# A two-block kernel whose expert stage runs in program order, gathers rows and streams through 22 tiles

## The chip, the core and the metric

One NeuronCore of a Trainium2 chip runs the whole program in one launch. The metric is device microseconds per execution: 1643.91 us in the median of 3 runs (1638.96 to 1644.89). The traced execution took 1639.19 us, 1637.3 us of it between its first and its last instruction (the span); every time of the trace below counts from the span's start.

## The reference

256 tokens of 1024 float32 numbers pass through two different blocks.

```python
# first block
u = rmsnorm(h) @ w_in;  h = h + concat(stick_breaking(u), rwkv7(u)) @ w_out
xn = rmsnorm(h)
# hier_moe: 1 of 4 groups by softmax, then 2 of its 8 experts, 32 experts in all
for e in range(32):
    y = y + combine[:, e:e+1] * ((silu(xn @ w_gate[e]) * (xn @ w_up[e])) @ w_down[e])
x = rmsnorm(h + y)
# second block, two layers of
x = x + 0.5 * swiglu(rms_norm(x), ffn1_w_gate, ffn1_w_up, ffn1_w_down)     # 1024 -> 2816 -> 1024
x = x + concat(ssd(...), mla(...), conv(...)) @ w_out
x = x + 0.5 * swiglu(rms_norm(x), ffn2_w_gate, ffn2_w_up, ffn2_w_down)
```

An expert's three weights are 1 MB each (1024x256, 1024x256, 256x1024), so the expert stage reads 96 MB.

## The kernel before

`Front` does the first block's mixers, `Moe` the experts, `Block2` the second block. Five engines run their own instruction lists: TensorE (PE, with its weight loads PEld), VectorE (DVE), ScalarE (ACT), GpSimd (POOL) and SyncE (SP), which issues the weight loads. The framework's scheduler orders each list by its own estimates. Instructions issued through `K.V`, `K.S`, `K.T` (class `InOrder`), or through `K.engines()` and `K.mm` while `K.ordered` is true, keep the order of the program text instead.

**Experts (`Moe.run`).** Each expert has room for 32 tokens (CAP), and four experts form a quad, so a quad's 4 x 32 places fill 128 partitions. `OH[j]` holds, for token half j, which token sits in which place (0 or 1). The 8 quads q go through these steps:

- gather: `gather(q, j, b)` multiplies token columns (stationary, every 8th column of `x`) by `OH` (moving, 128 columns), which gives the tokens of the quad already transposed; 16 matmuls a quad, each two instructions in the trace. `gathered(b)` scales them out of PSUM into `XG0` (DVE) and `XG1` (ACT, four pieces).
- `up(a, q, hf)`: 32 matmuls a half for the gate (hf 0) and for the up part (hf 1); k is the outer loop and the expert i the inner one, so that four neighbouring matmuls fill four different 32-column strips of the array.
- `act`: SiLU (ACT), times up and weight (DVE), two transposes (PE), copy to `hT` (ACT).
- `down(q, hT)`: 16 matmuls over two 512-column halves n, expert i outside, k inside.
- `back(q, ys, n)`: the result, split into `yh` (ACT) and `yl` (DVE), goes back to the tokens through `OHT` into four accumulators `py`. `slots_T` makes `OHT` for two quads at once, at even q.

Quad 0 also computes the routing weights (`weights`: 16 pairs of small matmuls on `cw` for all quads), `beyond` counts the fullest expert, and at q == 2 every engine branches on that count (`all_tokens`, not taken here).

**The ring.** `load_next` issues the 96 weight loads of 1 MB in order from SP (L1046, L1051, L1054): a quad's 4 gates, 4 ups, 4 downs. They go into NRING = 20 tiles; load n needs the tile of load n - 20 to be free. The first 20 wait only until `Front` gives its memory up; load 20 waits for `up(0)`'s gate half, and so on. A load also waits until the one 8 places before it has landed. `spare` takes ring tiles again for late use (`fg`, `fsq`, `yr`). Only the routing and quad 0 up to `act` are in program order (`K.ordered`).

**Gate/up of the second block (`Block2.ffn`, L1713).** Weights come as units of two 128-row slices k with 512 columns (256 gate, 256 up), split into `wh` (ACT) and `wl` (DVE). For every output half b and s (gate, up), `K.mm` issues two matmuls of `wh` with 512 moving columns and two of `wl` with 256: long, long, short, short, four times a unit. There are 10 such i with 4 units in each of 4 FFNs: 160 units, 1280 long and 1280 short matmuls.

Of the kernel before, what the change touches and what calls it, by code (L numbers as in the profile page):

```python
# [9 lines left out]
F32 = mybir.dt.float32  # L10
# [3 lines left out]
OP = mybir.AluOpType  # L14
# [939 lines left out]
        router.rest = [acs[1, n] for n in range(2)]  # L954


NRING = 20
BIG = 1e30


class Moe:
# [52 lines left out]
    def run(self, ctx, x, B=None):  # L1014
# [98 lines left out]
            return [lambda: K.V.tensor_add(rank[:, j], negm[:, j], pr[:, j]), lambda: place(j, 0, 4)]  # L1113


        XG, pg = [None, None], [None, None]
# [9 lines left out]
        def gathered(b):  # L1126
            XG[b] = wk.tile([P, 4, P], F32, name=f"XG{b}")
            if b == 0:
                K.V.tensor_mul(XG[b], pg[b], gp[:, 0:4, None].to_broadcast([P, 4, P]))
            else:  # L1130
                for k in range(4):
                    S.activation(XG[b][:, k], pg[b][:, k], AF.Copy, scale=gp[:, 4 + k:5 + k])
        OHT = [None]

        def slots_T(q):
            OHT[0] = wk.tile([P, 2, T], F32R, name="OHT")
            pt = K.mx.tile([P, 2, T], F32, name="mx")
            for i in range(2):
                for j in range(2):
                    nc.tensor.transpose(pt[:, i, j * P:(j + 1) * P],  # L1140
                                        OH[j][:, 4 * (q + i):4 * (q + i) + 4].rearrange("p e c -> p (e c)"), K.ident)
            S.activation(OHT[0], pt, AF.Copy)  # L1142

        def quads(t):
# [3 lines left out]
        def weights():  # L1148
            def t(name, n=1):
                return K.sm.tile([P, 2, n], F32, name=name, bufs=1)  # L1150
            eg, gs, p2, w1 = t("weg", 4), t("wgs"), t("wp2"), t("ww1")
            l32 = lm.rearrange("p j g e -> p j (g e)")
            K.V.tensor_sub(eg, lg[:, :, 0:4], mg.to_broadcast([P, 2, 4]))
            K.V.tensor_sub(p2, v8[:, :, 1:2], v8[:, :, 0:1])
            K.V.tensor_sub(l32, l32, v8[:, :, 0:1].to_broadcast([P, 2, NE]))
            S.activation(eg, eg, AF.Exp)
            S.activation(p2, p2, AF.Exp)
            S.activation(l32, l32, AF.Exp)
            V.tensor_reduce(gs, eg, axis=AX.X, op=OP.add)
# [6 lines left out]
            V.tensor_mul(comb, quads(mask), quads(l32))  # L1166
            for j in range(2):
                for q in range(8):
                    K.mm(pw[:, q], OH[j][:, 4 * q:4 * q + 4].rearrange("p e c -> p (e c)"), cw[:, j, q], j + q == 0, j == 1, share=True)
            V.tensor_mul(own, own, pw[:, :, 0:4])  # L1170
            V.tensor_reduce(ws[:, 0:8], own, axis=AX.X, op=OP.add)
            V.tensor_copy(ws[:, 8:16], pw[:, :, 4])


        def beyond():
# [49 lines left out]
        def down(q, hT):  # L1225
            ys = []
            for n in range(2):
                y = K.mx.tile([P, 512], F32, name="mx")
                for i in range(4):
                    for k in range(2):  # L1230
                        K.mm(y[32 * i:32 * i + 32], hT[:, k, 32 * i:32 * i + 32],
                             W["d", 4 * q + i, 0][:, k, n * 512:(n + 1) * 512], k == 0, k == 1)
                ys.append(y)
            return ys

# [10 lines left out]

        def back(q, ys, n):
            if q == 7 and n:
                t = spare("yr", 2, F32R)
# [34 lines left out]
        gather(0, 0, 0)  # L1284
        run(ranks(1))
        gather(0, 1, 0)
        gather(0, 0, 1)
        gathered(0)
        gather(0, 1, 1)
        for j in range(2):  # L1290
            place(j, 4, NE)
        def next_rows(q):
            for b in range(2):
                for j in range(2):
                    gather(q, j, b)
                gathered(b)

        for q in range(NE // 4):
            if q == 2:
                all_tokens(nmax)  # L1300
            if q == 2:
                next_rows(q)
            a = K.mx.tile([P, 1024], F32, name="mx")
            if q == 0:
                gathered(1)
            up(a, q, 0)
            load_next(4)
            if q == 7:
                fg = spare("fg", 17)
                src = A["final_norm_g"]  # L1310
                nc.gpsimd.dma_start(fg, bass.AP(tensor=src.tensor, offset=src.offset, ap=[[0, P], [1, D]]))
            up(a, q, 1)
            load_next(4)
            if q == 0:
                weights()
                nmax = beyond()
# [8 lines left out]
            if q == 0:  # L1325
                next_rows(1)
                K.ordered = False
            if q == 0:
                with_x(1, 1)
            if q == 7 and B:  # L1330
                next(par, None)
            y = down(q, hT)
            load_next(4)
            for n in range(1 if q == 7 else 2):
                back(q, y, n)


        V, S = K.V, K.S
        st = K.sm.tile([P, 2, 2, 2], F32, name="fst", bufs=1)
        a1 = K.sm.tile([P, 2], F32, name="fa", bufs=1)  # L1340
        sq = spare("fsq", 18)
        half = [slice(n * 512, (n + 1) * 512) for n in range(2)]

        def square(j, n):
# [37 lines left out]
    def act(self, wk, a, w, r):  # L1382
        K, nc = self.K, self.nc
        sg = wk.tile([P, 256], F32, name="msg")
        hT = wk.tile([P, 2, P], F32, name="mhT")
        nc.scalar.activation(sg, a[:, 0:256], AF.Silu, scale=r)
        nc.vector.scalar_tensor_tensor(sg, a[:, 256:512], w, sg, op0=OP.mult, op1=OP.mult)
        for k in range(2):
            nc.tensor.transpose(a[:, 512 + k * P:512 + (k + 1) * P], sg[:, k::2], K.ident)
        nc.scalar.activation(hT, a[:, 512:768].rearrange("p (k t) -> p k t", k=2), AF.Copy)  # L1390
        return hT


# [19 lines left out]
class Block2:  # L1413
# [258 lines left out]
    def ffn(self, ctx, x, first=None):  # L1672
# [40 lines left out]
        for i in range(1, FF // 256):  # L1713
            ac = sums(i)
            for wh, wl, k0, m in self.units(("gu", i), 0, KD):
                for b in range(2):
                    for s in range(2):
                        c = slice(s * 256 + b * P, s * 256 + (b + 1) * P)
                        for k in range(m):
                            K.mm(ac[b][s], wh[:, k, c], X[:, k0 + k], k0 + k == 0, False, share=True)  # L1720
                        for k in range(m):
                            K.mm(ac[b][s][:, 0], wl[:, k, c], X[:, k0 + k, 0], False, k0 + k == KD - 1, share=True)
# [615 lines left out]
```

## Time and profile before

| | |
|---|---|
| traced execution, and its span | 1639.19 us, 1637.3 us |
| PE busy | 1585.5 us, 97% of the span |
| DVE, ACT busy | 1032.5 us (63%), 832.0 us (51%) |
| first and last issue of an expert weight load | 163.01 us, 424.53 us |
| first and last matmul on expert weights | 236.85 us, 454.19 us |
| mean granted TensorE clock | 0.984 |

Busy times of PE count a matmul from its start to a modelled end, and matmuls overlap, so a busy PE may still be late or early: the distance from one start to the next is what a matmul takes of the engine. Idle time is listed with the engine that ended it. The transfer rate of each 41 us slice stands in the page's slices; 421 GB/s is the highest, held through three of them.

### The profile page before, as it was taken

To read this page: it belongs to the slowest core of one execution; us is meant where nothing else is said; L and a number is where in the kernel's file an instruction comes from. 1 tells how busy PE (TensorE), PEld (TensorE's weight loads), DVE (VectorE), ACT (ScalarE), POOL (GpSimd) and SP (SyncE) were. 2 spreads that over 40 slices of the span, in tenths; PEclk is the share of its full clock that TensorE was granted. 3 is DMA by queue.
4 is the path that set the end of the run, shared out by engine and by line. 5 is a ranking of instruction groups with operands and counts; after the bars stand their busy time and mean duration, and the time that the engine had idled before them with its cause. 6 is when DMAs were issued, how large, how long until landed. Compare 5 with 4: busy or idle time off the path is not lost.

```text
span 1637.3 us, 25206 instructions
## 1 busy us (share of the span) xinstructions
PE 1585.5 (97%) x9862; PEld 1325.9 (81%) x9862; DVE 1032.5 (63%) x1905; ACT 832.0 (51%) x1400; POOL 43.5 (3%) x134
## 2 busy tenths in 40 slices
PE   8999999999889999999999999999999999999998
PEld 7989875665458888899878888888888989778887
DVE  7876651000177656868987775667658779876753
ACT  6633421111255654668745664456546677555653
POOL 4000000000200000000000000000000000000000
PEclk9999999999999999999999999999999999999999
DMA  6431589999765555643545655566556434555553
GB/s 211 140 93 65 220 314 382 421 421 421 318 217 182 180 190 189 200 155 104 178 164 173 193 183 191 194 191 184 190 187 224 142 108 157 175 169 180 181 194 114
DMA packets 195644, 331.29 MB, mean 202 GB/s; under 512 B 11972, under 2 KB 150674, under 8 KB 183362
## 3 DMA queue, kind: packets, MB, share of 16 engines
q1 hardware_dynamic: 186208, 315.19, 55.5%
q0 software_dynamic: 4528, 13.41, 2.4%
q8 instruction: 78, 1.28, 0.3%
q10 hardware_dynamic: 4786, 1.05, 0.3%
q14 instruction: 44, 0.36, 0.1%
HBM read 328.25 MB, written 1.38 MB: 201 GB/s over the span
## 4 chain that ended last, share of the span: by engine, by line
PE 76%; DVE 3%; ACT 2%; issue 1%; DMA 0%; POOL 0%; ACTq 0%
PE acc L246 39%; PE mx L246 27%; PE acc L48 7%; DVE wl L258 1%; PE mx L48 1%; DVE wl L48 1%; DMA cr<-csd 0%; PE mx L1954 0%; PE mx L1978 0%; ACT wh L277 0%; ACT p L1969 0%; PE mx L2024 0%; ACT fsq L48 0%; ACT X L48 0%; DVE x L1520 0%
## 5 line engine op out<-in xcount | busy, mean ns | idle before, releaser
L258 DVE TENSOR_TENSOR wl<-wr,wh 128x1024 fp32r<-128x1024 f32 x358 | 436.3, 1222 | 255.9 <-ACT wh L277 255.2
L277 ACT ACTIVATE wh<-wr 128x1024 fp32r<-128x1024 f32 x358 | 377.8, 1058 | 335.2 <-PE acc L246 235.5
L246 PE MATMUL acc<-X,wh 128*128 128x256 f32 (+1 forms) x1664 | 396.5, 330 | 0.0
L246 PE MATMUL acc<-X,wl 128*128 128x256 f32 x1152 | 272.5, 282 | 0.0
L246 PEld LDWEIGHTS acc<-X,wh 128*128 128x128 f32 x1664 | 260.1, 191 | 5.3 <-issue 4.2
L246 PEld LDWEIGHTS acc<-X,wl 128*128 128x128 f32 x1152 | 218.5, 190 | 28.5
L246 PE MATMUL mx<-X,wh 128*128 128x512 f32 x640 | 201.6, 396 | 0.0
L246 PEld LDWEIGHTS mx<-X,wl 128*128 128x128 f32 x640 | 120.2, 188 | 28.4
L246 PE MATMUL mx<-X,wl 128*128 128x256 f32 x640 | 125.8, 278 | 0.0
L246 PE MATMUL acc<-wh,hh 128*128 128x512 f32 x288 | 112.1, 389 | 0.0
L246 PE MATMUL acc<-wl,hh 128*128 128x512 f32 x288 | 112.1, 389 | 0.0
L246 PE MATMUL acc<-wh,hl 128*128 128x512 f32 x288 | 112.0, 389 | 0.0
L246 PEld LDWEIGHTS mx<-X,wh 128*128 128x128 f32 x640 | 97.5, 189 | 0.2
L246 PEld LDWEIGHTS acc<-wh,hl 128*128 128x128 f32 x288 | 54.1, 188 | 11.2
L246 PEld LDWEIGHTS acc<-wh,hh 128*128 128x128 f32 x288 | 54.1, 188 | 11.1
L246 PEld LDWEIGHTS acc<-wl,hh 128*128 128x128 f32 x288 | 54.1, 188 | 11.1
L246 PE MATMUL acc<-wh,m 128*128 128x512 f32 x192 | 61.3, 394 | 0.0
L246 PE MATMUL mx<-mw,XG 128*32 128x256 f32 x896 | 58.1, 391 | 0.0
L1254 DVE TENSOR_TENSOR yl<-mx,yh 128x512 fp32r<-128x512 f32 x15 | 10.4, 691 | 75.0 <-ACT yh L1253 75.0
L246 PEld LDWEIGHTS mx<-OH,x 128*128 128x128 f32 x192 | 46.7, 334 | 7.8 <-issue 3.3
L246 PE MATMUL mx<-mw,mhT 128*32 128x512 f32 x256 | 48.3, 622 | 4.6 <-ACT mhT L1390 4.6
L246 PE MATMUL mx<-OH,x 128*128 128x128 f32 x192 | 49.3, 411 | 3.5 <-ACT OHT L1142 1.4
(643 smaller groups left out, 2609.2 us busy)
## 6 DMA issues: line engine op xcount, KB each, us to landing
wr<-in_w_in SPq DMA_DIRECT2D x44, 1024.0 KB, 5.3
wr<-in_ffn_w_gate SPq DMA_DIRECT2D x88, 512.0 KB, 4.0
wr<-in_ffn_w_up SPq DMA_DIRECT2D x88, 512.0 KB, 5.0
wr<-in_ffn_w_down SPq DMA_DIRECT2D x40, 1024.0 KB, 5.0
mw<-in_exp_w_gate SPq DMA_DIRECT2D x32, 1024.0 KB, 19.2
mw<-in_exp_w_up SPq DMA_DIRECT2D x32, 1024.0 KB, 17.8
mw<-in_exp_w_down SPq DMA_DIRECT2D x31, 1024.0 KB, 16.4
wr<-in_w_out SPq DMA_DIRECT2D x20, 1024.0 KB, 4.9
```

What stands on the lines that cost most here:

```text
L48: return lambda *a, **k: self.tc.keep_in_program_order(f(*a, **k))
L246: self.engines()[2].matmul(out, l, r, start=start, stop=stop, skip_group_check=share)
L258: i = self.K.engines()[0].tensor_sub(l, v, h)
L277: self.K.engines()[1].activation(h, v[:, q:q + c], AF.Copy)
L1254: K.engines()[0].tensor_sub(yl, ys[n], yh)
```

## The change

The expert stage stays in program order to its end (`K.ordered = False` moves behind the loop; `act` and `slots_T` go through `K.engines()` and `K.T`). The gather swaps operands: `OH` is stationary and 512 columns of `x` move, four matmuls a quad; `gathered` copies the rows to `xr` (half by ACT, half by DVE), and `rows_T` transposes them (8 PE transposes of every 8th column) and scales them into `XG0`, `XG1`. The gather for quad q + 1 stands ahead of `act(q)`, its `rows_T` behind it. `down` gets k outside and i inside. Quad 0 computes its own routing weights alone (`slot_weights(0, 1)`); the other seven, the count and one `with_x` follow its `down`. The ring has 22 tiles; the software queue's scratch shrinks to 4096 bytes of a partition. The FFN issues, for a unit, all 8 long matmuls and then all 8 short ones.

```diff
-NRING = 20
+NRING = 22
...
-        def gather(q, j, b):
+        def gather(q, j):
             if j == 0:
-                pg[b] = K.mx.tile([P, 4, P], F32, name="mx")
+                pg[0] = K.mx.tile([P, 2, 512], F32, name="mx")
+            for n in range(2):
+                K.mm(pg[0][:, n], OH[j][:, 4 * q:4 * q + 4].rearrange("p e c -> p (e c)"), x[:, j, n * 512:(n + 1) * 512],
+                     j == 0, j == 1, share=True)
+        def gathered():
+            xr[0] = wk.tile([P, 2, 512], F32, name="xr")
+            S.activation(xr[0][:, 0], pg[0][:, 0], AF.Copy)
+            V.tensor_copy(xr[0][:, 1], pg[0][:, 1])
+        def rows_T():
+            pt = K.mx.tile([P, KD, P], F32, name="mx")
+            for k in range(KD):
+                T_.transpose(pt[:, k], r[:, k::KD], K.ident)
...
+            V.tensor_mul(XG[0], pt[:, 0:4], gp[:, 0:4, None].to_broadcast([P, 4, P]))
             for k in range(4):
-                K.mm(pg[b][:, k], x[:, j, 4 * b + k::KD], OH[j][:, 4 * q:4 * q + 4].rearrange("p e c -> p (e c)"),
-                     j + k == 0, j == 1, share=True)
+                S.activation(XG[1][:, k], pt[:, 4 + k], AF.Copy, scale=gp[:, 4 + k:5 + k])
...
-                for i in range(4):
-                    for k in range(2):
+                for k in range(2):
+                    for i in range(4):
                         K.mm(y[32 * i:32 * i + 32], hT[:, k, 32 * i:32 * i + 32],
...
-            if q not in (0, 1, 7):
-                next_rows(q + 1)
+            if q != 7:
+                rows(q + 1)
...
             hT = self.act(wk, a, ws[:, q:q + 1], ws[:, 8 + q:9 + q])
-            if q == 0:
-                next_rows(1)
-                K.ordered = False
+            if q not in (1, 7):
+                rows_T()
...
+            if q == 0:
+                slot_weights(1, 8)
+                nmax = beyond()
+                with_x(1, 1)
...
+                bs = [(ac[b][s], slice(s * 256 + b * P, s * 256 + (b + 1) * P)) for b in range(2) for s in range(2)]
+                for a, c in bs:
+                    for k in range(m):
+                        K.mm(a, wh[:, k, c], X[:, k0 + k], k0 + k == 0, False, share=True)
+                for a, c in bs:
+                    for k in range(m):
+                        K.mm(a[:, 0], wl[:, k, c], X[:, k0 + k, 0], False, k0 + k == KD - 1, share=True)
...
+    nc = bacc.Bacc("TRN2", target_bir_lowering=False, num_devices=1, dynamic_dma_scratch_size=4096)
```

On SP, loads 19 to 22 of the ring before (`waits` names the semaphores: DMAHW of earlier loads, PE, DVE):

```order
L1046 DMA mw<-in_exp_w_up 128x2048 [waits DMAHW2_49]
L1051 DMA mw<-in_exp_w_down 128x2048 [waits DMAHW3_49,PE_49]
L1051 DMA mw<-in_exp_w_down 128x2048 [waits DMAHW4_49,PE_49]
L1051 DMA mw<-in_exp_w_down 128x2048 [waits DMAHW5_49,PE_49]
```

The same four loads of the change:

```order
L1046 DMA mw<-in_exp_w_up 128x2048 [waits DMAHW2_49]
L1051 DMA mw<-in_exp_w_down 128x2048 [waits DMAHW3_49,DVE_49]
L1051 DMA mw<-in_exp_w_down 128x2048 [waits DMAHW4_49]
L1051 DMA mw<-in_exp_w_down 128x2048 [waits DMAHW5_49,PE_49]
```

Loads 20 and 21 no longer wait for PE; the DVE wait of load 20 is for `Front`'s last write in that memory. From load 22 on PE frees the tiles.

On PE, quad 5 before, from its gate/up matmuls (`mw` the weights, `XG` the gathered tokens; `OH_2282`, `OH_2283` the two token halves) to its way back:

```order
L246 MATMUL mx<-mw,XG_3308 32x256 x15
L246 MATMUL mx<-mw,XG_3319 32x256 x16
L246 MATMUL mx<-mw,XG_3308 32x256 x16
L246 MATMUL mx<-mw,XG_3319 32x256 x16
L246 MATMUL mx<-OH_2282,x 128x128 x4
L246 MATMUL mx<-OH_2283,x 128x128 x4
L1389 MATMUL mx<-ident,msg 128x128 x2
L246 MATMUL mx<-mw,mhT 32x512 x16
L246 MATMUL acc<-yh,OHT 128x512 x2
L246 MATMUL acc<-yl,OHT 128x512 x2
```

The same stretch of the change (`xr` the gathered rows):

```order
L48 MATMUL mx<-mw,XG_3327 32x256 x16
L48 MATMUL mx<-mw,XG_3328 32x256 x16
L48 MATMUL mx<-mw,XG_3327 32x256 x16
L48 MATMUL mx<-mw,XG_3328 32x256 x16
L48 MATMUL mx<-x,OH_2288 128x512 x2
L48 MATMUL mx<-x,OH_2289 128x512 x2
L48 MATMUL mx<-ident,msg 128x128 x2
L48 MATMUL mx<-ident,xr 128x128 x8
L48 MATMUL mx<-mw,mhT 32x512 x16
L48 MATMUL acc<-yh,OHT 128x512 x2
L48 MATMUL acc<-yl,OHT 128x512 x2
```

Eight gather matmuls before the `msg` transposes (the other eight stand elsewhere) became four with 512 columns, and eight transposes follow the `msg` transposes.

In `Block2.ffn`, PE before (one and a half of the four (b, s) of a unit):

```order
L246 MATMUL acc<-X,wh 128x512 x2
L246 MATMUL acc<-X,wl 128x256 x2
L246 MATMUL acc<-X,wh 128x512 x2
```

and in the change, a whole unit and the start of the next:

```order
L246 MATMUL acc<-X,wh 128x512 x8
L246 MATMUL acc<-X,wl 128x256 x8
L246 MATMUL acc<-X,wh 128x512 x8
```

The matmuls are the same; the switches between long and short fall from eight to two a unit.

## Rows read from the trace of the kernel before

**Rows 1.** Page: PE's line, and the transfer rate of the 40 slices.
```profile
PE 1585.5 (97%) x9862; PEld 1325.9 (81%) x9862; DVE 1032.5 (63%) x1905; ACT 832.0 (51%) x1400; POOL 43.5 (3%) x134
...
GB/s 211 140 93 65 220 314 382 421 421 421 318 217 182 180 190 189 200 155 104 178 164 173 193 183 191 194 191 184 190 187 224 142 108 157 175 169 180 181 194 114
```

**Rows 2.** Busy by stretch: PE, PEld, DVE, ACT, POOL; then clock, DMA share, GB/s.
```profile
235.00:240.00 5.00, 4.27 (x41) 3.07 (x44) 2.49 (x12) 2.07 (x8) 0.00 (x0) 1.00 0.25 103
240.00:245.00 5.00, 5.00 (x100) 3.02 (x96) 0.03 (x1) 0.00 (x0) 0.00 (x0) 1.00 0.40 111
...
250.00:255.00 5.00, 4.29 (x13) 2.92 (x14) 1.23 (x6) 1.92 (x3) 0.00 (x0) 0.50 1.01 424
...
260.00:265.00 5.00, 5.00 (x35) 3.24 (x38) 0.00 (x0) 1.14 (x4) 0.00 (x0) 1.00 0.74 306
265.00:270.00 5.00, 4.78 (x23) 1.68 (x14) 1.38 (x2) 1.19 (x2) 0.00 (x0) 1.00 0.62 213
...
440.00:445.00 5.00, 4.80 (x88) 2.59 (x79) 0.00 (x0) 0.15 (x2) 0.00 (x0) 1.00 0.33 131
```

**Rows 3.** Timeline of SP, 160 to 300 us: start, length, and issues merged.
```profile
242.07 2.27 SPq L1051 DMA_DIRECT2D mw<-in_exp_w_down  x4
...
265.88 2.12 SPq L1046 DMA_DIRECT2D mw<-in_exp_w_up  x4
```

**Rows 4.** Timeline of PE in quads 2 and 5.
```profile
304.86 0.66 PE L1140 MATMUL mx<-ident,OH 128*128 128x128 f32 x4
...
314.89 3.68 PE L246 MATMUL mx<-mw,mhT 128*32 128x512 f32 x32
...
378.46 7.11 PE L246 MATMUL mx<-mw,XG 128*32 128x256 f32 x126
385.50 4.07 PE L246 MATMUL mx<-OH,x 128*128 128x128 f32 x16
...
391.08 7.11 PE L246 MATMUL mx<-mw,mhT 128*32 128x512 f32 x32 [1.28 <-ACT mhT L1390]
```

**Rows 5.** Groups by line, 290 to 430 us: count, busy us, mean ns, idle before.
```profile
L1253 ACT ACTIVATE yh<-mx 128x512 fp32r<-128x512 f32 x10 | 6.0, 597 | 27.0 <-PE mx L246 18.6 <-PE acc L246 8.4
...
L1387 DVE SCALAR_TENSOR_TENSOR msg<-mx,ws,msg 128x256 f32<-128x256 f32 x5 | 2.4, 481 | 22.7 <-ACT msg L1386 22.7
L1386 ACT ACTIVATE msg<-mx,ws 128x256 f32<-128x256 f32 x5 | 2.4, 475 | 47.9 <-PE mx L246 47.9
```

**Rows 6.** Timeline of PE in quad 0.
```profile
238.80 7.10 PE L48 MATMUL mx<-mw,XG 128*32 128x256 f32 x124
...
245.83 4.70 PE L48 MATMUL acc<-cw,OH 128*128 128x5 f32 x32
```

**Rows 7.** Timeline of PE at the end of the expert stage.
```profile
454.19 1.90 PE L246 MATMUL mx<-mw,mhT 128*32 128x512 f32 x4
...
456.78 1.46 PE L246 MATMUL acc<-yr,OHT 128*128 128x512 f32 x4 [0.26 <-ACT yr L1253]
462.67 1.94 PE L48 MATMUL mx<-ident,xn 128*128 128x128 f32 x8 [4.43 <-DVE xn L48]
```

**Rows 8.** Timeline of PE: Front at 60 us, gate/up at 520 us, down at 600 us.
```profile
60.08 0.28 PE L246 MATMUL acc<-xh,wh 128*128 128x256 f32 x1
...
62.48 0.28 PE L246 MATMUL acc<-xh,wl 128*128 128x256 f32 x1
...
519.90 0.63 PE L246 MATMUL mx<-X,wh 128*128 128x512 f32 x2
520.37 0.39 PE L246 MATMUL mx<-X,wl 128*128 128x256 f32 x2
...
525.47 0.63 PE L246 MATMUL acc<-X,wh 128*128 128x512 f32 x2
...
600.05 0.39 PE L246 MATMUL acc<-wl,hh 128*128 128x512 f32 x1
...
605.95 0.39 PE L246 MATMUL acc<-wh,hh 128*128 128x512 f32 x1
```

More of the change, by code (lines that the diff above doesn't have):

```diff
@@ L1113, in ranks @@
             return [lambda: K.V.tensor_add(rank[:, j], negm[:, j], pr[:, j]), lambda: place(j, 0, 4)]
-        XG, pg = [None, None], [None, None]
-        def gather(q, j, b):
+        XG, pg, xr = [None, None], [None], [None]
+        def gather(q, j):
             if j == 0:
-                pg[b] = K.mx.tile([P, 4, P], F32, name="mx")
-            for k in range(4):
-                K.mm(pg[b][:, k], x[:, j, 4 * b + k::KD], OH[j][:, 4 * q:4 * q + 4].rearrange("p e c -> p (e c)"),
-                     j + k == 0, j == 1, share=True)
[L1126 to L1132, printed above, removed]
+                pg[0] = K.mx.tile([P, 2, 512], F32, name="mx")
[4 more added lines that the diff above has]
+            xr[0] = wk.tile([P, 2, 512], F32, name="xr")
+            V, S, _ = K.engines()
+            S.activation(xr[0][:, 0], pg[0][:, 0], AF.Copy)
+            V.tensor_copy(xr[0][:, 1], pg[0][:, 1])
+        def rows_T():
+            pt = K.mx.tile([P, KD, P], F32, name="mx")
+            r = xr[0].rearrange("p n f -> p (n f)")
+            V, S, T_ = K.engines()
+            for k in range(KD):
+                T_.transpose(pt[:, k], r[:, k::KD], K.ident)
+            for b in range(2):
+                XG[b] = wk.tile([P, 4, P], F32, name=f"XG{b}")
+            V.tensor_mul(XG[0], pt[:, 0:4], gp[:, 0:4, None].to_broadcast([P, 4, P]))
+            for k in range(4):
+                S.activation(XG[1][:, k], pt[:, 4 + k], AF.Copy, scale=gp[:, 4 + k:5 + k])
         OHT = [None]
@@ L1139, in slots_T @@
                 for j in range(2):
-                    nc.tensor.transpose(pt[:, i, j * P:(j + 1) * P],
-                                        OH[j][:, 4 * (q + i):4 * (q + i) + 4].rearrange("p e c -> p (e c)"), K.ident)
+                    K.T.transpose(pt[:, i, j * P:(j + 1) * P],
+                                  OH[j][:, 4 * (q + i):4 * (q + i) + 4].rearrange("p e c -> p (e c)"), K.ident)
             S.activation(OHT[0], pt, AF.Copy)
@@ L1166, in weights, with slot_weights @@
             V.tensor_mul(comb, quads(mask), quads(l32))
+        def slot_weights(q0, q1):
             for j in range(2):
[L1168 to L1172, printed above, removed]
+                for q in range(q0, q1):
+                    K.mm(pw[:, q], OH[j][:, 4 * q:4 * q + 4].rearrange("p e c -> p (e c)"), cw[:, j, q], j == 0 and q == q0, j == 1, share=True)
+            V = K.V
+            V.tensor_mul(own[:, q0:q1], own[:, q0:q1], pw[:, q0:q1, 0:4])
+            V.tensor_reduce(ws[:, q0:q1], own[:, q0:q1], axis=AX.X, op=OP.add)
+            V.tensor_copy(ws[:, 8 + q0:8 + q1], pw[:, q0:q1, 4])
         def beyond():
@@ L1283, in run, with rows @@
         K.mm(pr[:, 1], lt, mask[:, 1], start=False, share=True)
-        gather(0, 0, 0)
+        gather(0, 0)
         run(ranks(1))
[L1286 to L1289, printed above, removed]
+        gather(0, 1)
+        gathered()
+        rows_T()
         for j in range(2):
             place(j, 4, NE)
[L1292 to L1296, printed above, removed]
+        def rows(q):
+            for j in range(2):
+                gather(q, j)
+            gathered()
         for q in range(NE // 4):
@@ L1301, in run @@
             if q == 2:
-                next_rows(q)
+                rows_T()
             a = K.mx.tile([P, 1024], F32, name="mx")
-            if q == 0:
-                gathered(1)
             up(a, q, 0)
@@ L1324, in run @@
             hT = self.act(wk, a, ws[:, q:q + 1], ws[:, 8 + q:9 + q])
-            if q == 0:
-                next_rows(1)
-                K.ordered = False
-            if q == 0:
-                with_x(1, 1)
+            if q not in (1, 7):
+                rows_T()
             if q == 7 and B:
@@ L1385, in act @@
         hT = wk.tile([P, 2, P], F32, name="mhT")
-        nc.scalar.activation(sg, a[:, 0:256], AF.Silu, scale=r)
-        nc.vector.scalar_tensor_tensor(sg, a[:, 256:512], w, sg, op0=OP.mult, op1=OP.mult)
+        V, S, T_ = K.engines()
+        S.activation(sg, a[:, 0:256], AF.Silu, scale=r)
+        V.scalar_tensor_tensor(sg, a[:, 256:512], w, sg, op0=OP.mult, op1=OP.mult)
         for k in range(2):
-            nc.tensor.transpose(a[:, 512 + k * P:512 + (k + 1) * P], sg[:, k::2], K.ident)
-        nc.scalar.activation(hT, a[:, 512:768].rearrange("p (k t) -> p k t", k=2), AF.Copy)
+            T_.transpose(a[:, 512 + k * P:512 + (k + 1) * P], sg[:, k::2], K.ident)
+        S.activation(hT, a[:, 512:768].rearrange("p (k t) -> p k t", k=2), AF.Copy)
         return hT
```

19 lines of the change are left out of this document (6 added, 13 removed).

## The prediction

> **What bounds the kernel now.** I read the page first. PE is busy 97% of the span, and the transfers stand at 421 GB/s for three slices and near it in two more [rows 1]: these slices are the expert stage, and there two limits lie close together. So I took that stage in stretches of 5 us, then its PE and SP lists, then its last microseconds.
>
> The stream of expert loads: at 421 GB/s a 1 MB tile takes 2.49 us, the 12 tiles of a quad 29.9 us. The stream is broken twice. From 235 to 245 us it moves 103 and 111 GB/s, from 260 to 270 us 306 and 213 [rows 2]. Against 421 that is (318 + 310) x 5 = 3140 KB, or 7.5 us, and (115 + 208) x 5 = 1615 KB, or 3.8 us. Both end with an SP issue [rows 3]: at 242.07, when `up(0)`'s gate half has freed the first ring tiles (its matmuls run from 238.80 [rows 6]), and at 265.88, when `down(0)` has freed its own. Then the stream runs full until 440 us; the 131 GB/s of the next 5 us are 1.6 us more, so the last byte lands at 441.6 [rows 2].
>
> PE ends the stage later: its last expert matmuls stop at 456.09, the last `back` at 458.24 [rows 7], 16.6 us after the last byte. From 270 us on PE is what is late. Quad 5 shows why: `up` 7.1 us, half a gather 4.07 (the whole 8.1), `down` 7.11 [rows 4], and `back`. `down` does the same work in 3.68 us in quad 2 [rows 4]: there four column strips run side by side, in quads 1 and 4 to 7 the written order keeps two.
>
> In the FFNs PE works without a gap, so a matmul is worth its distance to the next.
>
> **The change, part by part.**
>
> *PE's path in a quad.* Out go gather 8.1 us and, in five quads, a 7.1 us `down`; in come:
> - Gather, four f32 matmuls with 512 columns. `up` does 64 matmuls of 256 columns, four at a time, in 7.11 us [rows 4]: 0.44 us for one, 0.89 for 512 columns, 3.6 us for four.
> - Eight transposes with every 8th column as weights. Bounds: a contiguous one takes 0.66/4 = 0.165 us, one gather instruction with every 8th column of `x` as weights 4.07/16 = 0.254 [rows 4]. So 1.3 to 2.0 us; I take 2.0, the row with the same stride.
> - A new wait. In program order ACT copies `xr` (0.60 for 512 columns) ahead of SiLU (0.475), then DVE multiplies (0.48) [rows 5], and PE has nothing in between; with three handovers of some 0.2 us (an estimate) 2.2 us. Queued behind it on PE are the `msg` transposes, `rows_T` and `down`. Before, half a gather covered that chain. The copy to `hT` hides under `rows_T`, the scaling into `XG` under `down`.
> - `down`, k outside: always four strips, 3.7 us [rows 4]. `up` 7.1 stays, and `back`, eight matmuls at 0.227 [rows 8] and its waits, some 2.7; at even q, `slots_T` adds 0.66 [rows 4] and the wait for its copy (0.60 [rows 5]) 0.7.
>
> The sum is about 22 us a quad, 23.5 at even q. Quad 0 starts its `up` 1 to 2 us sooner (gather 3.6, copies 1.3 one behind the other, transposes 2.0, scaling 0.9, against 8.1 before [rows 4, 5]). The 4.70 us of small matmuls [rows 6] nearly all move behind `down(0)`. I place `down(0)`'s end at 259, quad 0's at 268, then q1 20, q2 27 (branch and an exposed `rows_T`), q3 22, q4 23.5, q5 22, q6 23.5, which ends at 406; with quad 7 PE alone would be done near 425.
>
> *The stream.* Loads 20 and 21 wait for no PE work any more and queue behind load 19: two tiles, 5.0 of the 7.5 us. Load 22 needs `up(0)`'s gate half, about 1.5 us sooner than 242.07, and some 0.5 us stay lost. Load 30 needs `down(0)`: 259 instead of 265.9, when the stream wants it at about 260, so the 3.8 us go. Load 34 needs `up(1)`'s gate half, which now stands behind the moved small matmuls: I see 271.6 against 270.4 wanted, a new loss of 1.2. Sum: 7.0 + 3.8 - 1.2 = 9.6 us; bounds 5.0 (only the two tiles) and 11.3 (both gaps whole). The last byte comes at 432.0. By then PE waits for tiles, with some 8 us in hand. Reordering POOL's `fg` and parameter loads costs nothing: the same bytes on the same engines. The 4096-byte scratch I price at 0: POOL issues a handful of loads in this stage. Were one held up, `fg`, 0.5 MB (1.3 us at the stream's rate), is wanted only at the end.
>
> *Behind the last byte.* Half of `down` (1.85 us) and the last way back (458.24 - 456.09 = 2.15 [rows 7]) are 4.0 us at full clock, 8 at half, since PE comes out of a wait of some 8 us before quad 7's up half. I take 6.5, in the middle: 438.5, that is 19.7 us before 458.24. Bounds: 16 (last byte 434, half clock) and 23 (430.3 and full clock). The 4.43 us wait that follows [rows 7] stays, as do its squares and norms. The next weights queue right behind the expert loads (two tiles, 437 at the latest) and are used 6 us after 438.5, so they are not late.
>
> *FFN.* Eight runs of long, long, short, short take 525.47 - 519.90 = 5.57 us, 0.696 a run; of one, the longs take 520.37 - 519.90 = 0.47. Long matmuls alone follow at 0.227 (26 distances from 600.05 to 605.95), short ones alone at 0.120 (20 from 60.08 to 62.48) [rows 8]: 2 x 0.227 + 2 x 0.120 = 0.694. So a pair of switches costs some 0.0025 us, a unit has four pairs and keeps one: 0.0075 x 160 units = 1.2 us. Bounds: if only the longs speed up to 0.227, (0.47 - 0.454) x 4 x 160 = -10; if only the shorts slow down from 0.113 to 0.120, +9. I take -1.5, by the uniform rows.
>
> Sum: -19.7 - 1.5 = -21.2 us on the profiled 1639.19, 1618.0. That execution lies at the lower end of the three runs, whose mean is 1642.6 and median 1643.91; from their mean 1621.4. I say **1621**.
>
> A rule bears on the short matmuls and the transposes. The Trainium skill, "TensorE: Matmul & The Clock Gate", section "LDWEIGHTS (loading the stationary operand)", has a weight load take its columns over 1.2 GHz, whatever their place: 107 ns for 128. By it the eight transposes would take 0.9 us, not 2.0, and the whole forecast not move, as PE waits there anyway; the gather's 0.254 us per instruction [rows 4] speaks for the stride. It also puts a short matmul's load just under the 120 ns at which short ones follow each other here [rows 8], so that runs of eight would be at the edge.
>
> **Rivals.**
>
> *PE stays the limit.* My 22 us a quad are drawn from rows, but PE now stands idle 2 to 3 us in every quad, and the granted clock has been at 0.50 behind such pauses: 250 to 255 us, after quad 0's small matmuls and a stall [rows 2]. If every quad loses 2.5 to 3.5 us (a drop of 5 us or a little more at 1.2 GHz), 425 becomes 443 to 450, past the stream: 8 to 15 us gained, 1626 to 1633 with the FFN; I set 1631. For it: an in-order list with new waits. Against it: the quads before had waits too, 1.28 us ahead of `down` in quad 5 [rows 4], and most ran at full clock. The Trainium skill, same page, Part 1, says the clock is gated down by default and activity releases it; by that rule, the trace agrees with its 0.50, and the pauses are this rival's trigger.
>
> *Slower: a run of eight short matmuls is bound by its weight loads.* The place is all 160 units. Now each pair of shorts comes behind two longs, which hide loads. If a run of eight could not hide them, a short would take what a contiguous transpose does, a load and 128 columns in 0.165 us [rows 4], instead of (0.696 - 0.47)/2 = 0.113 [rows 8]: 0.052 x 1280 = 67 us, so 1690. It decides from 0.129 us a short on (20/1280 = 0.016 above 0.113), where the experts' gain is eaten. Against it: Front's stream of 256 columns has new weights for each matmul and runs at 0.120 [rows 8].
>
> *Only part of it happens:* the two loads wait for memory that `Front` holds long, or the clock drops in the tail. 2.5 to 5 us less, 1624 to 1627; this is inside the forecast's range.
>
> **How the numbers follow.** The forecast (the stream ends the stage) gets 0.67 with its own range 1614 to 1628, PE as the limit 0.25, short matmuls bound by loads 0.04, something unseen that leaves the time where it is 0.04. What a measurement of this kernel can tell from no change is about 0.5%, 8 us: below 1635.7. Faster takes the forecast and most of the first rival: 0.90; same 0.06; slower 0.04. The range for 8 in 10 runs from 1612 to 1633: it adds most of the first rival and, below, both gaps closed whole and a better FFN.
>
> **What would show it.** In the trace after: SP issues loads 20 and 21 right behind 19, near 225 us; the rate stays above 400 GB/s from 210 to 430 us; `down` takes 3.7 us in each quad; PE waits for tiles in quads 6 and 7; the last `back` ends near 438; gate/up has longs at 0.227 and shorts at 0.12. I am wrong if the last `back` comes after 446, if PE never waits for tiles, or if shorts follow each other at more than 0.13.

## The result, and the profile after

The changed kernel takes 1624.59 us (median of 4 runs, 1623.43 to 1627.65), the kernel before 1643.76 beside it (1638.96 to 1644.89): ratio 0.9885, 95% interval 0.9857 to 0.9912. Run again with the last experiments it took 1626.54 (0.9904, 0.9882 to 0.9927). The forecast was 1621.

The page answers [rows 1]; three slices of the expert stage stay near 420 GB/s as before, the slices beside them rise from 314, 382 and 318 GB/s to 369, 388 and 374, and PE's share falls:

```profile
PE 1549.9 (95%) x9734; PEld 1283.6 (79%) x9734; DVE 1036.6 (64%) x1916; ACT 828.3 (51%) x1408; POOL 43.5 (3%) x134
...
GB/s 209 136 102 66 202 369 388 421 420 420 374 182 194 182 194 176 181 163 104 156 182 195 185 196 183 202 182 185 176 203 203 157 118 151 173 157 188 197 178 111
```

The stretches of [rows 2] but for the one from 250 us (columns as there), and those from 245, 270, 275 and 435 us. The hole of 103 and 111 GB/s is 433 and 342 now and goes on with 344, that of 306 and 213 is 421 and 423, and a new one of 380 and 290 stands from 270 to 280:

```profile
235.00:240.00 5.00, 2.80 (x41) 1.98 (x44) 3.06 (x4) 1.74 (x5) 0.00 (x0) 1.00 1.03 433
240.00:245.00 5.00, 5.00 (x100) 3.03 (x96) 2.01 (x12) 0.47 (x3) 0.00 (x0) 1.00 0.90 342
245.00:250.00 5.00, 4.31 (x27) 2.23 (x19) 0.38 (x3) 0.60 (x1) 0.00 (x0) 1.00 0.89 344
...
260.00:265.00 5.00, 4.44 (x40) 3.88 (x32) 0.66 (x4) 0.00 (x0) 0.00 (x0) 0.96 1.01 421
265.00:270.00 5.00, 4.72 (x9) 2.41 (x9) 0.95 (x3) 0.60 (x1) 0.00 (x0) 0.50 1.01 423
270.00:275.00 5.00, 5.00 (x71) 2.64 (x74) 0.07 (x1) 0.00 (x0) 0.00 (x0) 0.86 0.92 380
275.00:280.00 5.00, 5.00 (x68) 2.58 (x61) 0.00 (x0) 0.00 (x0) 0.00 (x0) 1.00 0.79 290
...
435.00:440.00 5.00, 4.39 (x28) 1.03 (x28) 0.69 (x1) 0.60 (x1) 0.00 (x0) 1.00 1.09 354
440.00:445.00 5.00, 2.42 (x9) 1.35 (x8) 3.63 (x9) 3.90 (x11) 0.00 (x0) 1.00 0.92 292
```

SP's issues, against [rows 3] (the merged length shows where an issue inside waited). Loads 20 and 21, the first two of the four at 226.81, go out behind 19; 22 waits in that row until 242.06. The `w_down` loads of quad 2 start at 261.46; the third of them, load 34, goes out at 274.98:

```profile
224.92 1.78 SPq L1046 DMA_DIRECT2D mw<-in_exp_w_up  x4
226.81 17.08 SPq L1051 DMA_DIRECT2D mw<-in_exp_w_down  x4
...
261.46 14.64 SPq L1051 DMA_DIRECT2D mw<-in_exp_w_down  x4
276.19 3.05 SPq L1046 DMA_DIRECT2D mw<-in_exp_w_gate  x4
```

PE, against [rows 4, 7, 8]: quad 5 whole, quad 6 waiting for its up tiles, the end of the stage, and a gate/up unit:

```profile
362.15 7.11 PE L48 MATMUL mx<-mw,XG 128*32 128x256 f32 x128
369.20 3.70 PE L48 MATMUL mx<-x,OH 128*128 128x512 f32 x8
374.70 0.51 PE L48 MATMUL mx<-ident,msg 128*128 128x128 f32 x2 [1.81 <-DVE msg L48]
375.05 1.06 PE L48 MATMUL mx<-ident,xr 128*128 128x128 f32 x8
376.04 3.95 PE L48 MATMUL mx<-mw,mhT 128*32 128x512 f32 x32
379.92 0.73 PE L48 MATMUL acc<-yh,OHT 128*128 128x512 f32 x2
...
382.73 4.08 PE L48 MATMUL mx<-mw,XG 128*32 128x256 f32 x66
388.14 0.62 PE L48 MATMUL mx<-mw,XG 128*32 128x256 f32 x2 [1.33 <-DMA mw<-in_exp_w_up]
390.62 0.88 PE L48 MATMUL mx<-mw,XG 128*32 128x256 f32 x2 [1.85 <-DMA mw<-in_exp_w_up]
394.19 5.34 PE L48 MATMUL mx<-mw,XG 128*32 128x256 f32 x58 [2.70 <-DMA mw<-in_exp_w_up]
...
436.65 3.62 PE L48 MATMUL mx<-mw,mhT 128*32 128x512 f32 x26 [0.32 <-DMA mw<-in_exp_w_down]
...
441.23 1.19 PE L246 MATMUL acc<-yr,OHT 128*128 128x512 f32 x4
447.96 1.94 PE L48 MATMUL mx<-ident,xn 128*128 128x128 f32 x8 [5.54 <-DVE xn L48]
...
504.01 2.00 PE L246 MATMUL mx<-X,wh 128*128 128x512 f32 x8
505.85 1.11 PE L246 MATMUL mx<-X,wl 128*128 128x256 f32 x8
```

Quad 5 is 382.73 - 362.15 = 20.6 us. From the start of `up` to the end of `down` it took 391.08 + 7.11 - 378.46 = 19.7 us before, with half a gather [rows 4]; now 376.04 + 3.95 - 362.15 = 17.8, with the whole gather and all transposes. The waits for DMA `mw` tiles in quads 6 and 7 are new (before, PE has none in the whole stage): the stream is the limit. The last `back` stops at 441.23 + 1.19 = 442.42, 4.4 us behind the last byte (437.98).

**Where the 19 us are.** The two profiled executions differ by 1637.3 - 1623.4 = 13.9 us only. The changed one reached its first gather 2.3 us later (231.35 against 229.06), in code that is the same: in `Front` the granted clock stood at its lower level longer. By stretches of 2 us from 90 to 98 us it is 0.84, 0.50, 0.81 and 1.00 before, 0.62, 0.50, 0.50 and 0.68 after: some 3.4 us at 0.50 against 6.8.

Over all traces of this study the first gather starts between 227.5 and 233.9 us; in the repeat of the change it was 227.6. So stages are compared from the first gather on. From there to the first `xn` transposes of the FFN: 233.6 us before, 216.6 and 217.1 with the change, 17 us less. Behind them 1174.6 us before, 1175.5 and 1173.7 after: nothing.

### The profile page after: what moved, and what is told of

Its sections match the earlier page's. It is cut to its first block, busy times and chain, and to the rows that moved or that the text cites. A ratio compares the mean times of both kernels' runs of the same rounds, so it can differ in the third digit from the quotient of the medians.

```text
span 1623.4 us, 25106 instructions
## 1 busy us (share of the span) xinstructions
PE 1549.9 (95%) x9734; PEld 1283.6 (79%) x9734; DVE 1036.6 (64%) x1916; ACT 828.3 (51%) x1408; POOL 43.5 (3%) x134
## 4 chain that ended last, share of the span: by engine, by line
PE 70%; DMA 6%; DVE 4%; ACT 2%; issue 1%; SPq 0%; ACTq 0%; DVEq 0%
PE acc L246 39%; PE mx L246 19%; PE acc L48 7%; PE mx L48 4%; DMA mw<-in_exp_w_down 2%; DMA mw<-in_exp_w_up 1%; DMA mw<-in_exp_w_gate 1%; DVE wl L258 1%; DVE wl L48 1%; PE mx L1969 0%; DMA wr<-in_w_in 0%; ACT wh L277 0%; PE mx L1993 0%; DMA wr<-in_ffn_w_up 0%; DVE ul L258 0%
## 5 line engine op out<-in xcount | busy, mean ns | idle before, releaser
L246 PE MATMUL acc<-X,wh 128*128 128x256 f32 (+1 forms) x1664 | 357.1, 329 | 0.0
L246 PEld LDWEIGHTS acc<-X,wh 128*128 128x128 f32 x1664 | 277.2, 191 | 25.4 <-issue 4.2
L246 PE MATMUL acc<-X,wl 128*128 128x256 f32 x1152 | 237.2, 284 | 0.0
L246 PEld LDWEIGHTS acc<-X,wl 128*128 128x128 f32 x1152 | 186.3, 191 | 6.9
L246 PE MATMUL mx<-X,wh 128*128 128x512 f32 x640 | 161.9, 393 | 0.0
L246 PEld LDWEIGHTS mx<-X,wl 128*128 128x128 f32 x640 | 88.3, 190 | 7.0
L246 PE MATMUL mx<-X,wl 128*128 128x256 f32 x640 | 90.5, 282 | 0.0
L48 PEld LDWEIGHTS mx<-mw,XG 128*32 128x32 f32 x1024 | 34.2, 114 | 37.9 <-issue 9.2
L246 PEld LDWEIGHTS acc<-wh,hl 128*128 128x128 f32 x288 | 54.1, 188 | 11.3
L246 PE MATMUL acc<-xh,wh 128*128 128x256 f32 x176 | 50.3, 286 | 0.0
L246 PE MATMUL acc<-xh,wl 128*128 128x256 f32 x176 | 49.9, 283 | 0.0
```

What stands on the lines that cost most here:

```text
L48: return lambda *a, **k: self.tc.keep_in_program_order(f(*a, **k))
L246: self.engines()[2].matmul(out, l, r, start=start, stop=stop, skip_group_check=share)
```

## The experiments

Each row is one kernel's median with its ratio to the kernel before run beside it; then, from its trace, three stretches: first gather to last byte of the stream, last byte to the end of the last `back`, first gather to the `xn` transposes.

| kernel | time, us | ratio (95%) | byte | behind | stage |
|---|---|---|---|---|---|
| before | 1643.0 to 1647.1 | 1 | 213.0 | 16.2 | 233.6 |
| change | 1624.6, 1626.5 | 0.9885, 0.9904 | 206.6, 207.1 | 4.4, 4.4 | 216.6, 217.1 |
| before + FFN order | 1641.5 | 0.9992 (0.9977-1.0007) | 211.5 | 20.2 | 236.1 |
| before + ring | 1634.1 | 0.9941 (0.9925-0.9958) | 208.3 | 16.8 | 229.9 |
| before + k outside | 1631.9 | 0.9913 (0.9885-0.9941) | 214.0 | 4.5 | 223.7 |
| before + k outside + ring | 1630.1 | 0.9923 (0.9900-0.9946) | 210.0 | 4.4 | 219.9 |
| program order alone | 1629.0 | 0.9922 (0.9894-0.9949) | 211.8 | 4.6 | 221.6 |
| change, ring 20 | 1626.7 | 0.9897 (0.9880-0.9913) | 210.5 | 4.5 | 220.1 |
| change, FFN of before | 1623.2 | 0.9879 (0.9855-0.9904) | 206.3 | 5.6 | 217.4 |
| change, `down` loops of before | 1623.9 | 0.9862 (0.9824-0.9901) | 206.8 | 4.4 | 216.8 |
| change, gather of before | 1627.1 | 0.9896 (0.9864-0.9928) | 207.0 | 5.5 | 218.0 |
| change, scheduler from quad 1 | 1626.7 | 0.9898 (0.9865-0.9932) | 211.1 | 4.5 | 221.1 |
| change + four edits | 1623.5 | 0.9883 (0.9858-0.9907) | 204.5 | 6.3 | 216.7 |

The column "behind" falls into two groups: 16 to 20 us where PE is late, 4.4 to 6.3 where the stream holds PE up or both end together.

**The FFN's order, alone and taken back.**

```diff
+                for a, c in bs:            # 8 long
+                    for k in range(m): K.mm(a, wh[:, k, c], X[:, k0 + k], ...)
+                for a, c in bs:            # then 8 short
+                    for k in range(m): K.mm(a[:, 0], wl[:, k, c], X[:, k0 + k, 0], ...)
```

> The kernel before with one edit: the FFN's gate/up matmuls of a unit as 8 long, then 8 short. Theory A (the expert stage carries the whole gain, the FFN nothing): between the two traces the sum of the distances of gate/up matmuls is 445.8 us before and 446.5 after, so the time stays within 2 us of the kernel before, and the distances come out at 231 (long) and 119 ns (short). My prediction's own term: 1.5 us faster. Rival B (the regrouping carries a good part of the 19 us): 5 us faster or more.

> The changed kernel with the FFN's gate/up order of before (2 long, 2 short). Theory A: nothing, within 1.5 us of the changed kernel's 1624.6 (0.6 us faster by the sum of distances). My prediction's own term: 1.5 us slower. Rival B (regrouping is part of the gain): 5 us slower or more.

Rival B falls in both: neither way moves the time by 5 us. The times (1.8 us under the kernel before beside it, 1.4 under the change) lie within A's bounds, but can't tell A from my own term of 1.5 us. The distances can: over all gate/up matmuls they sum up to 445.8 us in the old order (both kernels with it) and 446.4 to 446.5 in the new one (both with it): longs go from 233.6 to 230.5 ns on the mean, shorts from 115.4 to 119.0.

**The ring alone, and the change without it.**

```diff
-NRING = 20
+NRING = 22
```

> The kernel before with the ring of 22 tiles, the scratch of 4096 bytes and the three spare slots of the change, and nothing else. Theory A (before the change PE, not the stream, ends the expert stage): loads 20 and 21 are issued some 15 us sooner and the last byte lands 4 to 5 us sooner, but the last expert matmul does not move by more than 2 us, and the time stays within 3 us of the kernel before. Rival B (the stream of loads set the end all along, and the two tiles are the gain): 5 us faster or more.

> The changed kernel with the ring set back to 20 tiles (spare slots as before; scratch stays 4096). Theory A (after the change the stream ends the stage, 4.4 us behind its last byte): load 20 waits again for up(0)'s gate half, tiles 20 on land 4 us later, load 32 then waits for up(1)'s gate half and loses 1 us more; the last byte and the last back come 5 us later, the time is 1630. Rival B (PE sets the end, the two tiles are only early): within 1.5 us of the changed kernel, 1625.

The ring alone gave some 9 us, so A's "within 3 us" failed; but B's reason isn't it either. The last byte came 4.7 us sooner, and PE's end stayed 16.8 us behind it. What moved is PE's list: with the other ring the scheduler placed quad 4 otherwise. There `down` took 7.31 us before (partly at the lower clock), behind a gather cut in pieces; with the ring:

```profile
352.24 3.98 PE L246 MATMUL mx<-OH,x 128*128 128x128 f32 x16
356.05 0.27 PE L1389 MATMUL mx<-ident,msg 128*128 128x128 f32 x1
356.80 4.07 PE L246 MATMUL mx<-OH,x 128*128 128x128 f32 x16 [0.47 <-ACT mhT L1390]
360.80 3.68 PE L246 MATMUL mx<-mw,mhT 128*32 128x512 f32 x32
```

That quad is 7.9 us shorter (23.8 against 31.7 us from `up` to `up`) and the next one 3.2 longer (its `down` ran 8.77 us, with the clock low). The stage is 3.7 us shorter than in the trace of before, 6.2 shorter than in that of the FFN's order alone, which has the stage of before; the rest of the 9 us isn't resolved. In the change, taking the two tiles back moves the last byte 3.4 to 3.8 us, against 5 expected; the time, 2.1 us more, is within what a measurement here can tell.

**The loops of `down`, taken back and alone.**

```diff
-                for i in range(4):
-                    for k in range(2):
+                for k in range(2):
+                    for i in range(4):
                         K.mm(y[32 * i:32 * i + 32], hT[:, k, 32 * i:32 * i + 32],
-                             W[...], k == 0, k == 1)
+                             W[...], k == 0, k == 1, share=True)
```

(`W[...]` is shortened; `share` is handed on as `skip_group_check`.) The first run takes this edit back in the change, the second makes it alone in the kernel before.

> The changed kernel with the loops of down as before (the four experts outside, k inside), still in program order. Theory A (PE's shorter way through a quad is what moved the end from PE to the stream): a down takes 7.1 us again instead of 3.7 to 4.4, 3.4 us a quad, 27 us over eight quads. Against it stand the waits for tiles of the changed kernel, some 16 us on PE by its quads 6 and 7; so PE ends the stage again, 8 to 11 us later than with the change, and the time is 1633 to 1636, with no wait for tiles left in quads 6 and 7. Rival (the loads decide, PE has room for this): within 3 us of 1624.6.

> The kernel before with one edit: k outside and the four experts inside in down, so that four strips run side by side in every quad. Theory A: 3.4 us less in quads 1 and 4 to 7, 17 us on PE; the last byte stays at 442 us of before's trace, or up to 2 us sooner, and the stage ends some 5 us behind it, so the stream takes over: 10 to 12 us faster than before, 1631 to 1634. Rival (another part of PE's way takes the room, or the loads are late for another reason): under 4 us.

The first miss is the most telling one: with the old loops in program order `down` takes 3.98 us in quads 3 to 6, not 7.1. So the time fits the rival (1623.9), but the 27 us that were to test PE's room never came. The weight loads show what differs (one row for each group that starts together). Kernel before, quad 5, then the change with the old loops, quad 3:

```profile
391.08 0.15 PEld L246 LDWEIGHTS mx<-mw,mhT 128*32 128x32 f32 x4 [1.47 <-ACT mhT L1390]
391.54 0.12 PEld L246 LDWEIGHTS mx<-mw,mhT 128*32 128x32 f32 x2 [0.31 <-issue]
391.97 0.12 PEld L246 LDWEIGHTS mx<-mw,mhT 128*32 128x32 f32 x2 [0.30 <-issue]
...
392.82 0.15 PEld L246 LDWEIGHTS mx<-mw,mhT 128*32 128x32 f32 x5 [0.32 <-issue]
...
396.32 0.11 PEld L246 LDWEIGHTS mx<-mw,mhT 128*32 128x32 f32 x1 [0.32 <-issue]
396.75 0.11 PEld L246 LDWEIGHTS mx<-mw,mhT 128*32 128x32 f32 x1 [0.32 <-issue]
```

```profile
332.96 0.18 PEld L48 LDWEIGHTS mx<-mw,mhT 128*32 128x32 f32 x8
333.41 0.15 PEld L48 LDWEIGHTS mx<-mw,mhT 128*32 128x32 f32 x4 [0.28 <-issue]
333.84 0.15 PEld L48 LDWEIGHTS mx<-mw,mhT 128*32 128x32 f32 x4 [0.28 <-issue]
```

Four strips at each step of 0.43 us against two or three, and at the end one alone. In program order the matmuls of one column half (n) stand together: strips 0, 0, 1, 1, 2, 2, 3, 3, then the other half. In quad 5 before, the program on PE's list has strip and half mixed: 0 and 1 of the first half, 0 of the second, 2 of the first, 1 and 2 of the second, and both halves of 3 last. Strip 2 begins only at 392.82, when the first sum of strip 0 is through, and strip 3's two sums run one behind the other. So it wasn't the written order that kept two strips: the same loops took 3.68 us in quad 2 before [rows 4] and in quad 4 with the ring alone. What differs in the slow quads is the scheduler's mixture of the halves. The price was right all the same: k outside alone, still under the scheduler, gives 3.7 us at full clock and puts PE's end 4.5 us behind the last byte. Its last `down` loads weights as their tiles land:

```profile
388.02 3.68 PE L246 MATMUL mx<-mw,mhT 128*32 128x512 f32 x32 [1.28 <-ACT mhT L1390]
...
441.43 5.64 PE L246 MATMUL mx<-mw,mhT 128*32 128x512 f32 x32 [0.47 <-ACT mhT L1390]
...
442.17 0.27 PEld L246 LDWEIGHTS mx<-mw,mhT 128*32 128x32 f32 x4 [0.16 <-DMA mw<-in_exp_w_down]
...
443.45 0.15 PEld L246 LDWEIGHTS mx<-mw,mhT 128*32 128x32 f32 x7 [0.28 <-DMA mw<-in_exp_w_down]
...
448.04 1.19 PE L246 MATMUL acc<-yr,OHT 128*128 128x512 f32 x4
```

The time, 1631.9, is the one expected. It lies 15 us under the kernel before beside it, 3 to 5 more than expected; the stage is 10 us shorter than in the trace of before.

**The gather of before, and the scheduler's order, in the change.**

```diff
-            K.mm(pg[0][:, n], OH[j]..., x[:, j, n * 512:(n + 1) * 512], ...)   # 4 a quad, then xr, rows_T
+            K.mm(pg[0][:, k], x[:, j, k::KD], OH[j]..., ...)                   # 16 a quad
```

> The changed kernel with the gather of before: 16 matmuls with every 8th column of x as weights (7.9 us) instead of four with 512 columns, no copies to xr and no eight transposes; the scaling into XG stands where it stood; for quad 2 the gather follows the branch. Theory A: 7.9 against 3.7 + 1.1 + some 0.7 of wait, 2.4 us a quad, 8 us exposed at quad 2 and 1.5 at quad 0: 20 us more PE work, 16 of them under the waits for tiles, so 2 to 6 us slower than the change, 1627 to 1631. Rival (gather is free, PE waits anyway): within 1 us of 1624.6. Rival (gather was the main thing): 10 us slower or more.

```diff
+            if q == 0:
+                K.ordered = False
```

> The changed kernel with program order up to the end of quad 0 alone, and the scheduler's order from quad 1 on (it puts the gather for the next quad between the two msg transposes, so it covers the SiLU chain, and the first up matmuls between the way back). Theory A (what counts is the work on PE, and the stream ends the stage): the same within 2 us, 1624.6, the last byte within 1 us of the change's. Rival (program order itself is the gain): 5 us slower or more.

With the old gather quads 3 to 5 take 22.0, 23.4 and 22.0 us against 20.6, 21.9 and 20.6, some 1.4 more, since the long gather covers the SiLU chain that leaves PE idle for 1.81 us in the change; PE's room swallows it. The last byte stays, the stage is 0.9 to 1.4 us longer, the time 0.6 to 2.5: between A and the rival in which the gather is free this decides nothing; the rival of 10 us falls. With the scheduler's order quads 2 to 4 (21.3, 20.3, 21.7 us) are as short as in the change; the stage loses 4 us elsewhere: the scheduler puts quad 2's gather ahead of most of `up(1)`, so load 34 goes out at 276.45, 48.0 us behind the first gather instead of 43.6, and the last byte comes 4.0 to 4.5 us later, where A had it within 1. Of the time, at most 2 us are left.

**Two edits, and program order alone.** The first is the kernel before with k outside and the ring of 22; the second is the change with the ring, gather, `down` loops and FFN of before (quad 0's own slot weights and the scratch stay as changed).

> The kernel before with two edits: k outside in down, and the ring of 22 tiles (scratch and spare slots with it). New theory A2 (any edit that ends the 7.1 us downs hands the end of the stage to the stream, and the ring then takes out of the stream what it can; the rest of the change is worth little): the last byte comes some 3 us sooner than with k outside alone, 15 to 18 us faster than before, within 3 us of the changed kernel. Rival (the gather and program order carry their own part, 5 us or more): 5 us slower than the changed kernel or more.

> The changed kernel with everything undone but program order (and quad 0's own slot weights): ring of 20, the gather of before, the four experts outside in down, the FFN of before; the scratch stays 4096. Theory A2: in program order down keeps one column half at a time and takes 4.0 us whichever loop is outside, so this alone moves the end to the stream: 10 to 14 us faster than before, 4 to 7 us slower than the whole change. Rival (program order is worth nothing without the shorter gather and the ring): within 4 us of before.

Both move PE's end to 4.4 and 4.6 us behind the last byte. In the first PE waits for a tile inside the last `down`, as with k outside alone; in the second the last `down` runs whole in 3.68 us at 442.31, with no wait, so there PE and the stream end together. The ring's part: k outside with the ring brings the byte 4.0 us sooner than k outside alone. They lie 3.6 and 2.4 us above the change run beside them (1626.5) and 13 and 14 us under before. So A2 is met by program order alone against before, but it lost less to the change than the 4 to 7 expected, and with ranges that overlap (1624.7 to 1635.5, 1620.1 to 1627.4); for the two edits neither side is met cleanly: what is left for gather and order is about 3 us of the stage (219.9 against 217), not 5 or more.

**Four edits on top of the change.** `held` are quad 0's scaled rows of the second column half.

```diff
+            if q == 1:          # behind up(a, 1, 0)
+                slot_weights(1, 8); nmax = beyond(); with_x(1, 1); spread(0, 1, *held)
+            if q == 7:
+                kni = [(k, n, i) for i in range(4) for n in range(2) for k in range(2)]
-        next_gain()
+        next_gain(K.nc.sync)
-        square(1, 0)            # to the place behind square_x(0, 1)
```

> The changed kernel with four edits behind the reading of its trace: quad 0's second way back and the seven small slot-weight sets behind up(1)'s gate half, so that load 34 isn't late (1.0 us); the first FFN's gain row on SP, behind the expert loads, instead of on POOL among them (0.5 MB, 1.25 us); in quad 7 down with the experts outside and both column halves inside, so that only the last expert's four matmuls stand behind the last byte (1.2 us); ACT's squares of the first token half ahead of the others (0.5 us). Theory A2 (stream and tail set the stage): 3 to 4 us faster than the changed kernel run beside it. Rival (nothing of it is on the path): within 1 us.

> The changed kernel once more, beside the other three on the same chip, as their yardstick. Every theory: 1624.6 us, within 2 us. Its trace tells how far the start of the stage moves from one execution to the next: if Front's 2.3 us more in the first trace of the change belong to that execution and not to the change, its first gather starts within 1 us of the 229.1 us of before.

The yardstick's trace confirms that `Front`'s 2.3 us belonged to one execution (first gather at 227.60). The four edits gave 1623.5 against 1626.5, with ranges that overlap (1620.9 to 1626.4, 1620.1 to 1627.4): no gain can be claimed. The trace says why not 4 us: load 34 goes out in time and the last byte comes 2.1 to 2.6 us sooner, but the last `down`, now expert by expert, needs longer behind it (4.1 us to 442.37, before the edits 2.2):

```profile
433.58 8.86 PE L48 MATMUL mx<-mw,mhT 128*32 128x512 f32 x32 [0.47 <-ACT mhT L48]
442.37 0.73 PE L48 MATMUL acc<-yh,OHT 128*128 128x512 f32 x2
```

Its order, expert by expert with both halves inside, mixes the halves like the slow quads before, and here by the written program: at full clock the 32 records take 8.86 us, though no weight load in it waits for a tile, where the change's order needs 3.95 in quad 5. Of 1.2 us to be saved it made 1.9 lost.

## Why the prediction was right, and where it was not

**Bound.** Right: PE was late, the stream close behind. The ring alone left PE's end where it was relative to the last byte; k outside alone, or program order alone, cut "behind" from 16 to 4.5. In the change PE waits for tiles in quads 6 and 7, and it does so though the granted clock was low in parts of quads 0, 1, 6 and 7 (0.50 from 265 to 270 us), so the rival in which PE stays the limit fell. Of the signs named ahead, loads 20 and 21, the waits for tiles and the distances in gate/up came as said. Not so the rate, which falls below 400 GB/s in four stretches (342, 344, 380, 290), `down`, which takes 3.95 us in quads 3 to 5 and more at the lower clock, and the last `back`, which ends at 442.4 instead of 438, 2.3 us of it `Front`'s.

**The 7.1 us `down`.** Price right, cause wrong: "the written order keeps two" fell with the old loops in program order (3.98 us). With program order the loop swap is worth nothing here (216.8 against 216.6 and 217.1).

**PE's path.** Gather 3.70 (3.6), `down` 3.95 (3.7), `back` 2.8 (2.7), odd quads 20.6 (22). The wait was 1.81 (2.2). No row showed the 0.2 us for a handover: in quad 5 ACT's copy (0.60), DVE's copy of the other half (0.69, which I left out and under which SiLU ends) and the multiply (0.47) make 1.76 of the 1.81. The eight transposes took 1.06 us, not 2.0: my row with the same stride was a record of the gather, a matmul that leaves two records, and not of a transpose. `Front`'s eight contiguous transposes take 1.07 us in the trace of before (222.41), so the stride costs nothing. By the formula of the Trainium skill, "TensorE: Matmul & The Clock Gate", section "LDWEIGHTS (loading the stationary operand)", only the number of columns counts; the estimate from it for eight, 0.9 us, lies closer to the trace's 1.06 than mine did. PE had room, so it moved nothing.

**The stream.** From the first gather on, `down(0)` was to end after 29.9 us and ended after 29.2 (30.4 in the repeat); load 34 was to go out after 42.5 and did after 43.6. The step of the sum that was mis-sized is how much of the two holes closes: of 11.3 us, 9.6 were to go and 1.7 to stay. Counted in the same way, from 235 to 290 us, the four stretches under 400 GB/s above leave (79 + 77 + 41 + 131) x 5 = 1640 KB, 3.9 us; in the repeat 5.6 are left, most of them at load 34:

```profile
235.00:240.00 5.00, 5.00 (x100) 3.00 (x93) 3.26 (x13) 1.27 (x7) 0.00 (x0) 1.00 0.84 306
...
270.00:275.00 5.00, 5.00 (x93) 2.88 (x82) 0.00 (x0) 0.00 (x0) 0.00 (x0) 1.00 0.58 206
275.00:280.00 5.00, 3.42 (x8) 1.15 (x7) 0.92 (x2) 0.96 (x2) 0.00 (x0) 1.00 0.89 333
```

So 7.4 and 5.7 us went, and the last byte came 6.4 and 5.9 sooner. With the four edits, where load 34 goes out in time, 1.7 us are left, 2.2 less than in the first trace of the change, and the last byte comes 2.1 us sooner than there. The landing of tile 34 misleads here: it came 9.2 us sooner in both traces (57.87 against 48.67 us behind the first gather), but before it had more loads ahead of it (12.3 us from issue to landing, 5.0 in the change).

The first FFN's gain row, 0.5 MB on POOL's queue (1.25 us at 421 GB/s), was issued at 438.99, as the stream ended, and now goes out at 423.72, among its last tiles. The prediction said of POOL's loads that their order costs nothing because the bytes are the same; it asked how many, not whether they come before the last tile or behind it. What that costs isn't shown. With the four edits the row goes behind the expert loads, but from the first gather to the last byte as much is moved as in the change, 84.9 MB (415 GB/s over 204.5 us, 411 over 206.6): the FFN's first weights, which SP issues from 421.57 on in the change and only at 450.62 before, also run beside the last tiles. Up to 1.0 us between the holes and the last byte stays open; single tiles land 0.5 to 1.6 us late, at other places each time (tile 87 in the first trace of the change, 3.99 us behind 86 with 409 GB/s; tile 75 before, 3.82 behind 74 with 416).

**Behind the last byte.** 6.5 was taken between 4.0 and 8; the end came at full clock, 4.4. The wait that follows was to stay at 4.43 and is 5.54: the first scaling of `x` by the final norm's row no longer fits under `down`. Together: -6.4 - 11.7 + 1.1 = -17.0 us from first gather to `xn`, where -19.7 was predicted.

**FFN.** -1.5 was taken, +0.6 measured: shorts at 119.0 instead of 115.4 ns eat the longs' gain. The rival of shorts held up by their weight loads had the right sign at the right place, and 3.6 ns instead of 52; whether it is the weight loads isn't shown.

**The time.** The profiled execution of before, on which the sum was made, lay at the lower end of that kernel's runs (1635.5 to 1651.6 over the study), and the stage alone took 2.5 us longer in the other trace that has the same stage. So 17 us in the stage and 19.2 (16.5 in the repeat) between medians do not contradict each other; the last 1 to 2 us are not resolved. That 1621 came within 4 us is in part luck: stage and FFN were to give 21.2 us and gave 16.4 in the traces, and the medians first measured lie 2.8 us further apart than that. The scratch of 4096 bytes and quad 0's own slot weights have no run of their own.

## What to carry to other kernels

When two limits lie close together, the gains of edits don't add: here each of several single edits takes PE out of the way, and any one of them can then be taken back at 0 to 2.5 us of the time, 0 to 4.5 of the stage. Read for each trace how far the last matmul ends behind the last byte: here that number tells a late PE (16 us) from the rest. Near 4.4 look also whether the last `down` waits for a tile, since PE and the stream may end together. And count a stream by the holes in its rate, not by when one tile lands. And compare stages from a common event inside the trace, since what runs ahead of them can move by more than the edit.

## What had not been expected of the hardware

- Four strips of 32 columns run side by side even where each strip's matmuls stand in pairs one behind the other (3.98 us for 32 records); with the second half's sums mixed in among the first's the same work took 7.1 us, and 8.86 us in a written order that takes both halves expert by expert. Which of the mixed orders are slow is not settled: under the scheduler with k outside they are mixed too, and take 3.7.
- The distance of short matmuls depends on what stands around them: 115.4 ns on the mean in pairs behind longs, 119.0 in runs of eight; longs 233.6 and 230.5.
- With `Front`'s code and the inputs unchanged, the time to the first gather varied by 6.4 us between the traces of this study (227.5 to 233.9), by 3.8 between two traces of the same kernel (231.35 and 227.60).
